# A two-layer trunk in f32 on one core: SBUF tiles moved to multiples of 512 bytes, the pool maps multiplied in plain f32, and late parts, sums and turns placed behind the blocks that follow

## The chip, the cores and the metric

The kernel runs on one core of one Trainium2 chip. The metric is the device time of one execution in microseconds (us), as the median of several runs. The other numbers come from one profiled execution of the same program, in which every engine's instructions carry a start and a duration.

## The reference, cut to what matters

256 tokens of 2048 channels pass through two layers. All of it is f32.

```
x += pool_mixer(rms_norm(x))          # 4 groups of 512 channels: trailing mean minus token, 512x512 map, scale
x += mlp(rms_norm(x))                 # layer 0: 2048 -> 8192, squared relu, 8192 -> 2048
k, v = rms_norm(x) @ w_kv             # 2048 -> 4096
x += attention(rms_norm(x) @ w_q, k, v) @ w_o   # 16 heads of 128, stick-breaking, strictly causal
x += mlp(rms_norm(x))                 # layer 1
return rms_norm(x)
```

## The kernel before, in words

**Products in parts.** A matmul in the format f32r, which keeps fewer bits of an f32 number, is one record in the trace, where a matmul in plain f32 is two. Each f32 value is therefore held as a high part and a low part, and a product is three matmuls: high by high, low by high, high by low. One token tile of 128 rows against 512 weight columns is one matmul; in most products the activations are the stationary operand (loaded into the array, 128 columns) and the weights are the moving one (512 columns). `by_token` (L264) does this for plain products: L271, L273 and L274 are the three matmuls. In `product` (L459, L461, L463) and `whole` (L507, L509, L510) they are the same three for the up product of the MLP.

**Weights.** Every block of weights is 512x512 f32 (1 MB), loaded by a DMA into a `raw` tile or into one of four `chain` tiles (c0, c1, d0, d1), cast to its high part by ScalarE (L194) and subtracted to its low part by VectorE (L195). `hi` and `lo` have three buffers each. `next_block` hands out the next block; loads and splits run ahead of it. The four chain tiles also hold activations where no chain of weights needs them: the parts for K, Q and V, some parts for the up product (d1), and in the head the parts of the pool mixer's input.

**Stages.** The head (pool mixer) does four products of one block each (`product_a(..., groups=1)`), mixes each with a band matrix over the tokens (`mixed`, L625 and L627, plain f32), makes the parts for the up product (`Fast.make`) and turns the stream to token rows (`by_tokens`, L640). Then `mlp` walks the plan of `stage_plan`: group 0 has eight whole blocks U; groups 1 to 7 have the blocks P of a fast product of seven sums in place of eight (stationary tiles fh and fl), with the turns T (transposes of the hidden values to ht0 and ht1, squared) and the down blocks D of the group before; the last group has only T and D, and after each finished chunk of 512 channels the norm that follows takes that chunk (`follow.take(n)`: squares, transposes L333, parts). Then come the K and Q products (`product_w`, here the weights are the stationary operand), V, the attention as side work between blocks, the O product (16 blocks with oT0 to oT3 stationary, `norm1.take(n)` after each chunk), layer 1's MLP and the last norm.

**Order.** Each engine runs its instructions in program order; a scheduler places side work and the split of later blocks between the matmuls, and semaphores hold an instruction until what it reads is there. The SP queue issues nearly all weight loads; loads that add onto a chain tile are issued by GpSimd.

**Tile addresses.** Tiles are laid in each partition one after another, in the order in which the pools are opened, so a small tile moves every tile that follows. From the order and the sizes of the pools, the addresses modulo 512 bytes are: 96 for raw, chain, hi, lo and the stream xr; 256 for what lies behind them on the left (ht0, ht1, the c tiles, oT, attention); 480 for the pools on the right (fh, fl, the last norm). Pieces inside these tiles lie at multiples of 512 bytes, so each stationary piece has its tile's offset.

Of the kernel before, what the change touches and what calls it, by code (L numbers as in the profile page):

```python
# [35 lines left out]
WARM = 12  # L36
# [34 lines left out]
def trunk_kernel(ctx: ExitStack, tc: tile.TileContext, xt_in, band, cols, pool_w, up_w, down_w,  # L71
# [13 lines left out]
    small = ctx.enter_context(tc.tile_pool(name="small", bufs=1))  # L85
    ps_w = ctx.enter_context(tc.tile_pool(name="ps_w", bufs=4, space=PSUM))
# [28 lines left out]
    eps = const.tile([P, 1], F32, name="eps")  # L115
# [12 lines left out]

    for g in range(NCH):
        block(pool_w[g])  # L130
# [33 lines left out]
    def load():  # L164
# [5 lines left out]
        if base is None:  # L170
            raw = wide(tag) if tag else wraw.tile([P, KT, NB], F32, name="raw")
            step = KT // 2 if i < NCH else KT
            for k in range(0, KT, step):
                nc.sync.dma_start(raw[:, k:k + step, :], src[:, k:k + step, :])
# [9 lines left out]
    def split():  # L184
# [6 lines left out]
        if gain is None:  # L191
            step = KT // 2 if i < NCH else KT
            for k in range(0, KT, step):
                nc.scalar.copy(out=hi[:, k:k + step, :], in_=raw[:, k:k + step, :])  # L194
                nc.vector.tensor_tensor(out=lo[:, k:k + step, :], in0=raw[:, k:k + step, :],  # L195
                                        in1=hi[:, k:k + step, :].bitcast(F32), op=ALU.subtract)
# [111 lines left out]
    class Norm:  # L308
        def __init__(self):
            self.parts = [None] * NCH  # L310
            self.ss = small.tile([P, NT, NCH], F32, name="ss", bufs=2)
# [24 lines left out]
        def rows(self):  # L336

            total = small.tile([P, NT], F32, name="total")
# [34 lines left out]
    class Fast(Norm):  # L373
# [3 lines left out]
        def __init__(self, gain, new_bank):  # L377
            super().__init__()
            self.gain, self.new_bank, self.pools = gain, new_bank, []

# [4 lines left out]
        def make(self, n, src=None):  # L385

# [7 lines left out]
            tiles = []  # L394
            for half in range(2):
                if src is None:
                    bank = self.turned(n, half, (0, 1))
                for k in range(2):
                    c = 2 * half + k
                    gs = gt[:, self.gain, n * KT + c:n * KT + c + 1]  # L400
                    if src is None:
                        x = bank[:, :, k, :]
                    else:
                        x = src[:, c, :].rearrange("p (t s) -> p t s", t=NT)
                    tiles.append((half, k, x, gs))
                    to = [(x, hi[:, 1:3, k, :], lo[:, 1:3, k, :])] if half else [
                        (x[:, 0], hi[:, 0, k, :], lo[:, 0, k, :]),
                        (x[:, 1], self.other[:, n, 0, k, :], self.other[:, n, 1, k, :])]
                    for x, h, l in to:
                        nc.scalar.activation(out=h, in_=x, func=AF.Copy, scale=gs)  # L410
                        nc.vector.scalar_tensor_tensor(out=l, in0=x, scalar=gs, in1=h.bitcast(F32),
                                                       op0=ALU.mult, op1=ALU.subtract)

            f = wide(("c0", "c1", "d0", "c0")[n]).rearrange("p a (b k s) -> p (a b) k s", b=2, k=2)
            for half, k, x, gs in tiles:
                nc.scalar.activation(out=f[:, 2 * half:2 * half + 2, k, :], in_=x, func=AF.Copy,
                                     scale=gs)
# [18 lines left out]
    def mlp(layer, norm, following):  # L436

        with scope(name=f"h{layer}", bufs=1) as hp, scope(name=f"ev{layer}", bufs=1) as ev, \
                scope(name=f"ps_s{layer}", bufs=1, space=PSUM) as ps_s:
            spare = cycle(("turn", "x", "y", "z"))  # L440
            new_bank = lambda: ps_s.tile([P, NB], F32, name=next(spare))
# [3 lines left out]
            def product(i, part):  # L445
# [22 lines left out]
                def new(name):  # L468
                    u[name] = hp.tile([P, NB], F32, name=f"c{name}")
                    return u[name]  # L470

                def relu(name):
                    t = int(name[1]) - 1
                    nc.scalar.activation(out=u[name], in_=u[name], func=AF.Relu,
                                         scale=r[:, t:t + 1])
# [16 lines left out]
            def whole(i, j, part):  # L492
# [7 lines left out]
                for t in range(NT):  # L500
# [11 lines left out]
                    if ends:  # L512
                        c = u[f"{i + 1}{t + 1}"] = hp.tile([P, NB], F32, name=f"c{i + 1}{t + 1}")
                        nc.scalar.activation(out=c, in_=b, func=AF.Relu, scale=norm.r[:, t:t + 1])

            def turn(i):

                a, ks = i // 2, slice(2 * (i % 2), 2 * (i % 2) + 2)
                if i % 2 == 0:
                    h[a] = hp.tile([P, KT, 2 * S], F32R, name=f"ht{a}")  # L520
                b = ps_s.tile([P, NB], F32, name="turn").rearrange("p (k s) -> p k s", k=2)
# [6 lines left out]
                q = ev.tile([P, 2, S], F32, name="q")  # L528
# [4 lines left out]
            def down(n, part, follow):  # L533
# [3 lines left out]
                if part == 1:  # L537
# [3 lines left out]
                    if follow is not None:  # L541
                        follow.take(n)

            r = norm.r
            for g in range(NG + 1):
# [4 lines left out]
                for what, *at in stage_plan(g):  # L550
                    if what == "P":
                        product(*at)
                    elif what == "T":
                        turn(*at)
# [8 lines left out]
    with scope(name="ps_p", bufs=1, space=PSUM) as ps_m:  # L563
        new_bank = lambda: ps_m.tile([P, NB], F32, name="turn", bufs=2)
        norm = Fast(G["mlp0"], new_bank)
        pools = [tc.alloc_tile_pool(name=f"xs{n}", bufs=1, reuse_waits="tile")
                 for n in reversed(range(2, NCH))]
# [360 lines left out]
```

## Time and profile before

| | |
|---|---|
| median of 3 runs | 1886.88 us (1886.84 to 1887.16) |
| profiled execution, whole | 1889.27 us |
| its span, first to last instruction | 1887.6 us |
| TensorE busy | 1842.6 us (98%), 8360 records |
| VectorE, ScalarE, GpSimd busy | 70%, 58%, 5% |
| mean granted TensorE clock | 0.987 of full speed |

A record of the profile is one matmul as the engine runs it: a plain f32 matmul has two records, an f32r one has one. The busy time of TensorE says little by itself, since matmuls overlap in the pipe; what counts is the time from one matmul's start to the next one's. The granted clock of a stretch is 1.00 at 2.4 GHz and 0.50 at 1.2 GHz.

### The profile page before, as it was taken

The page shows a single profiled execution, that of the slowest core. Times are in us where ns is not written, and L with a number is a line of the kernel's source. Part 1 is how long each engine was busy: PE and PEld are TensorE (multiplying, and loading weights), DVE is VectorE, ACT ScalarE, POOL GpSimd, SP SyncE. Part 2 cuts the span into 40 slices and gives each one's busy share as a digit, 9 for nine tenths or more (in the row PEclk, how much of TensorE's full clock was granted, in tenths as well). Part 3 has the DMA queues.
Part 4 walks back from the last instruction along what each step waited for, and adds up shares of the span by engine and source line. Part 5 has one row for each costly group of instructions (what it writes and reads, how often), then busy time and mean ns, then how long its engine had stood idle before and what let it go on. Part 6 is the DMA issues. An engine that isn't in the chain of part 4 may idle for free.

```text
span 1887.6 us, 20963 instructions
## 1 busy us (share of the span) xinstructions
PE 1842.6 (98%) x8360; PEld 1494.1 (79%) x8360; DVE 1312.1 (70%) x1134; ACT 1089.5 (58%) x1137; POOL 92.6 (5%) x125
## 2 busy tenths in 40 slices
PE   7899999999999999999999998999999999999987
PEld 5788888888888887888888786888888888888875
DVE  7676777778787765666766566577786877777753
ACT  7655656656565654565665555556565656656553
POOL 0000100000000100000000100000000100000000
PEclk8999999999999998999999999999999999999998
DMA  7479888888879764555445455697979888888741
GB/s 285 138 188 298 195 287 206 271 245 245 257 211 286 200 202 159 179 170 174 169 163 188 159 173 210 192 256 223 268 207 303 191 286 203 278 244 242 183 178 67
DMA packets 57697, 404.85 MB, mean 214 GB/s; under 512 B 6528, under 2 KB 6784, under 8 KB 9472
## 3 DMA queue, kind: packets, MB, share of 16 engines
q1 hardware_dynamic: 45504, 315.44, 46.6%
q0 software_dynamic: 12096, 88.09, 24.4%
q8 instruction: 65, 1.06, 0.2%
q14 instruction: 32, 0.26, 0.0%
HBM read 401.40 MB, written 2.10 MB: 214 GB/s over the span
## 4 chain that ended last, share of the span: by engine, by line
PE 94%; DVE 2%; ACT 1%; issue 1%; DMA 0%; SPq 0%; POOL 0%; DVEq 0%; ACTq 0%; POOLq 0%
PE bank L273 16%; PE bank L271 16%; PE bank L274 16%; PE bank L237 6%; PE x L459 4%; PE x L461 4%; PE x L463 4%; PE bank L242 3%; PE z L463 3%; PE y L463 3%; PE y L461 3%; PE y L459 3%; PE z L461 3%; PE z L459 3%; PE turn L525 2%
## 5 line engine op out<-in xcount | busy, mean ns | idle before, releaser
L195 DVE TENSOR_TENSOR lo<-raw,hi 128x2048 fp32r<-128x2048 f32 (+1 forms) x196 | 440.5, 2247 | 278.8 <-ACT hi L194 278.8
L194 ACT CAST hi<-raw 128x2048 fp32r<-128x2048 f32 (+1 forms) x196 | 367.7, 1876 | 344.7 <-PE bank L273 229.6
L274 PE MATMUL bank<-lo,ht 128*128 128x512 f32 x1024 | 407.9, 398 | 0.0
L271 PE MATMUL bank<-hi,ht 128*128 128x512 f32 x1024 | 405.8, 397 | 1.4 <-ACT ht L527 1.4
L273 PE MATMUL bank<-hi,ht 128*128 128x512 f32 x1024 | 406.7, 397 | 0.0
L195 DVE TENSOR_TENSOR lo<-c,hi 128x2048 fp32r<-128x2048 f32 x112 | 256.5, 2290 | 61.0 <-ACT hi L194 61.0
L194 ACT CAST hi<-c 128x2048 fp32r<-128x2048 f32 x112 | 214.4, 1914 | 134.2 <-PE bank L273 44.4
L273 PEld LDWEIGHTS bank<-hi,ht 128*128 128x128 f32 x1024 | 193.2, 189 | 51.3 <-DVE ht L530 3.6
L271 PEld LDWEIGHTS bank<-hi,ht 128*128 128x128 f32 x1024 | 193.7, 189 | 47.9 <-ACT ht L527 2.2
L274 PEld LDWEIGHTS bank<-lo,ht 128*128 128x128 f32 x1024 | 193.0, 188 | 44.8
L202 DVE SCALAR_TENSOR_TENSOR lo<-raw,gt,hi 128x512 fp32r<-128x512 f32 x192 | 135.4, 753 | 78.0 <-ACT hi L201 77.5
L201 ACT ACTIVATE hi<-raw,gt 128x512 fp32r<-128x512 f32 x192 | 126.0, 715 | 97.0 <-PE bank L237 49.4
L194 ACT CAST hi<-d 128x2048 fp32r<-128x2048 f32 x56 | 107.0, 1911 | 98.9 <-PE bank L273 78.2
L195 DVE TENSOR_TENSOR lo<-d,hi 128x2048 fp32r<-128x2048 f32 x56 | 128.4, 2292 | 45.6 <-ACT hi L194 45.6
L461 PE MATMUL x<-hi,fl 128*128 128x512 f32 x336 | 133.7, 398 | 0.0
L459 PE MATMUL x<-hi,fh 128*128 128x512 f32 x336 | 133.7, 398 | 0.0
L463 PE MATMUL x<-lo,fh 128*128 128x512 f32 x336 | 133.0, 396 | 0.0
L539 DVE TENSOR_TENSOR xr<-bank,xr 128x512 f32<-128x512 f32 x128 | 88.0, 687 | 51.0 <-PE bank L274 51.0
L180 POOL DMA_DIRECT2D c<-in_up_w x56 | 48.5, 866 | 923.5 <-DVE lo L195 876.1
L237 PE MATMUL bank<-d,hi 128*128 128x512 f32 x256 | 90.3, 396 | 0.0
L459 PE MATMUL z<-hi,fh 128*128 128x512 f32 x224 | 90.3, 403 | 0.0
L237 PE MATMUL bank<-c,hi 128*128 128x512 f32 x256 | 89.0, 396 | 0.0
(248 smaller groups left out, 2856.7 us busy)
## 6 DMA issues: line engine op xcount, KB each, us to landing
raw<-in_down_w SPq DMA_DIRECT2D x128, 1024.0 KB, 5.0
c<-in_up_w POOLq DMA_DIRECT2D x56, 1024.0 KB, 10.4
raw<-in_up_w SPq DMA_DIRECT2D x44, 1024.0 KB, 5.4
c<-in_up_w SPq DMA_DIRECT2D x28, 1024.0 KB, 5.0
d<-in_up_w SPq DMA_DIRECT2D x28, 1024.0 KB, 7.5
d<-in_up_w POOLq DMA_DIRECT2D x28, 1024.0 KB, 8.6
raw<-in_k_w SPq DMA_DIRECT2D x16, 1024.0 KB, 4.8
raw<-in_q_w SPq DMA_DIRECT2D x16, 1024.0 KB, 4.8
```

The source lines that it names most:

```text
L194: nc.scalar.copy(out=hi[:, k:k + step, :], in_=raw[:, k:k + step, :])
L195: nc.vector.tensor_tensor(out=lo[:, k:k + step, :], in0=raw[:, k:k + step, :], in1=hi[:, k:k + step, :].bitcast(F32), op=ALU.subtract)
L201: nc.scalar.activation(out=hi[:, k, :], in_=raw[:, k, :], func=AF.Copy, scale=gs)
L202: nc.vector.scalar_tensor_tensor(out=lo[:, k, :], in0=raw[:, k, :], scalar=gs, in1=hi[:, k, :].bitcast(F32), op0=ALU.mult, op1=ALU.subtract)
L237: nc.tensor.matmul(banks[j], lhsT=hi[:, k, cols], rhs=a, start=first, stop=last)
L271: nc.tensor.matmul(banks[t], lhsT=a_hi, rhs=hi[:, k, :], start=first and k == 0, stop=False)
L273: nc.tensor.matmul(banks[t], lhsT=a_lo, rhs=hi[:, k, :], start=False, stop=False)
L274: nc.tensor.matmul(banks[t], lhsT=a_hi, rhs=lo[:, k, :], start=False, stop=last and k == KT - 1)
L459: nc.tensor.matmul(b, lhsT=ah, rhs=wh, start=begins and kg == 0 and k == 0, stop=False, skip_group_check=True)
L461: nc.tensor.matmul(b, lhsT=al, rhs=wh, start=False, stop=False, skip_group_check=True)
L463: nc.tensor.matmul(b, lhsT=ah, rhs=wl, start=False, stop=ends, skip_group_check=True)
L539: nc.vector.tensor_tensor(out=chunk(t, n), in0=bank["d"][t], in1=chunk(t, n), op=ALU.add)
```

## The change

- **Addresses.** `eps` is a piece of a tile of 448 bytes, `ss` and `total` are pieces of tiles of 128 and 192 bytes, and a tile of 480 bytes (`edge`) stands at the right end. By the order and sizes of the pools, raw, chain, hi, lo, xr, ht, oT, the attention's tiles, fh and fl then all begin at multiples of 512 bytes. The constants (ident, ones) stay where they were.
- **Pool maps.** The product of a group with its map is plain f32: 8 matmuls of 512 columns (L672) in place of 24 in parts. The map is loaded straight into a buffer of `hi` or `lo`. The casts and subtractions of map and stream go; the stream is scaled by the norm's gain in 16 VectorE instructions (`gained`). 16 warm-up matmuls stand in place of 12.
- **Head.** `Fast.make` becomes `quarters` (four evacuations into f, three casts, three subtractions) and `sums`. Chunks 2 and 3 are mixed behind U000 (`rest`), and turned to token rows behind U010 (`tokens_of_rest`).
- **Last group of a layer.** The turns go through four banks in rotation (turn, x, y, z) in place of one, and the plan is T0 T1 D00 T2 T3 D01.
- **The last chunk of a norm.** In layer 0 `follow.take(3)` becomes side work behind the block that follows; in layer 1 `norm1.take(3)` becomes side work behind U000. The banks of PSUM change hands at `end_of_attention` for that.

```diff
-        order = "T2 T3 T0 T1 D00 D01 D10 D11 D20 D21 D30 D31"
+        order = "T0 T1 D00 T2 T3 D01 D10 D11 D20 D21 D30 D31"
...
+    edge = ctx.enter_context(tc.tile_pool(name="edge", bufs=1, side="right"))
+    nc.vector.memset(edge.tile([P, EDGE], F32, name="edge"), 0.0)
...
-    eps = const.tile([P, 1], F32, name="eps")
+    eps = const.tile([P, 112], F32, name="eps")[:, 0:1]
...
+        def quarters(self, n, src=None):
...
+            f = self.f[n] = wide(self.homes[n]).rearrange("p a (b k s) -> p (a b) k s", b=2, k=2)
...
+                    nc.scalar.activation(out=f[:, 2 * half:2 * half + 2, k, :], in_=x, func=AF.Copy,
+                                         scale=gt[:, self.gain, n * KT + c:n * KT + c + 1])
+            for h, l, x in ((hi[:, 0], lo[:, 0], f[:, 0]),
+                            (self.other[:, n, 0], self.other[:, n, 1], f[:, 1]),
+                            (hi[:, 1:3], lo[:, 1:3], f[:, 2:4])):
+                nc.scalar.copy(out=h, in_=x)
+                nc.vector.tensor_tensor(out=l, in0=x, in1=h.bitcast(F32), op=ALU.subtract)
...
-                b = ps_s.tile([P, NB], F32, name="turn").rearrange("p (k s) -> p k s", k=2)
+                b = new_bank() if last else ps_s.tile([P, NB], F32, name="turn")
...
-                    if follow is not None:
+                    if follow is not None and n == NCH - 1 and layer == 0:
+                        side.append([lambda: follow.take(n)])
+                    elif follow is not None:
                         follow.take(n)
...
+    def load_map(g):
+        pool, name = ((whi, "hi"), (wlo, "lo"))[g % 2]
+        w[g] = pool.tile([P, KT, NB], F32, name=name)
+        step = KT // 2
+        for k in range(0, KT, step):
+            nc.sync.dma_start(w[g][:, k:k + step, :], pool_w[g, :, k:k + step, :])
+
+    def product(g):
+
+        ys[g] = [pp.tile([P, NB], F32, name=f"y{t}") for t in range(NT)]
+        for t in range(NT):
+            bank = ps_w.tile([P, NB], F32, name="bank")
+            for k in range(KT):
+                nc.tensor.matmul(bank, lhsT=xg[g][:, k, t * P:(t + 1) * P], rhs=w[g][:, k, :],
+                                 start=k == 0, stop=k == KT - 1)
+            nc.scalar.copy(out=ys[g][t], in_=bank)
...
+    product(0)
+    scaled_bands()
+    product(1)
+    mixed(0)
+    norm.sums(0)
+    product(2)
+    mixed(1)
+    norm.sums(1)
+    by_tokens(0)
+    product(3)
+    by_tokens(1)
+    early.release()
...
+    side.extend([[rest], [tokens_of_rest]])
...
+    side.append([lambda: norm1.take(NCH - 1)])
```

Three places show how instructions move on TensorE. A row gives the line, the operation, what it writes and reads, and the semaphores it waits for (DVE is VectorE, Activation is ScalarE).

The first is the end of the head. Before, the last band products (mix) and turns (xs) of chunks 2 and 3 stand ahead of the first block U000, which is the row L507:

```order
L625 MATMUL mix_569<-bands_135,y0_409 128x256 [waits DVE_49]
L627 MATMUL mix_569<-bands_135,y1_410 128x128
L640 MATMUL turn_620<-ident_85,xs_130 128x128
L640 MATMUL turn_626<-ident_85,xs_130 128x128 [waits Activation_49]
L640 MATMUL turn_626<-ident_85,xs_130 128x128 x2
L640 MATMUL turn_620<-ident_85,xs_130 128x128 [waits DVE_49]
L640 MATMUL turn_626<-ident_85,xs_130 128x128
L507 MATMUL x_659<-hi_334,fh_384 128x512
```

Now the turns of chunk 1 (xs1) are the last ahead of U000 (L516), and chunk 2's band products (L634, into z and turn) stand behind its 24 matmuls:

```order
L672 MATMUL bank_369<-lo_166,c1_149 128x512 x3
L649 MATMUL z_375<-ident_90,xs1_146 128x128 [waits Activation_49]
...
L649 MATMUL turn_381<-ident_90,xs1_146 128x128 [waits Activation_49]
...
L516 MATMUL x_392<-hi_394,fh_276 128x512
L518 MATMUL x_392<-hi_394,fl_277 128x512
...
L634 MATMUL z_440<-bands_141,y0_295 128x256 [waits Activation_49]
L636 MATMUL z_440<-bands_141,y1_296 128x128
L634 MATMUL turn_447<-bands_141,y0_295 128x256 [waits Activation_49]
...
L516 MATMUL x_392<-hi_400,fh_276 128x512
```

What moved is the work of two of the four chunks: it stands behind a block that does not read it.

The second place is the last group of layer 0, right after block D31 of the group before. Before, all turns write the one bank `turn`, and a turn waits for ScalarE to have read the one ahead:

```order
L274 MATMUL bank_4715<-lo_4748,ht1_4259 128x512
L525 MATMUL turn_4823<-ident_85,c21_4314 128x128 [waits PE_49]
...
L525 MATMUL turn_4832<-ident_85,c21_4314 128x128 [waits PE_49,Activation_49]
...
L525 MATMUL turn_4842<-ident_85,c11_4371 128x128 [waits PE_49,Activation_49]
...
L271 MATMUL bank_4860<-hi_4765,ht0_4841 128x512 [waits Activation_49]
L271 MATMUL bank_4861<-hi_4765,ht0_4841 128x512
L271 MATMUL bank_4947<-hi_4862,ht0_4841 128x512 [waits DVE_49]
L525 MATMUL turn_4851<-ident_85,c11_4371 128x128 [waits PE_49,Activation_49]
```

Now the four turns write four banks, one behind the other, and D00 follows (L267 and L269 are its first two kinds of matmul, high and low part of ht0):

```order
L270 MATMUL bank_4583<-lo_4616,ht1_4127 128x512
L536 MATMUL turn_4691<-ident_90,c11_4239 128x128 [waits PE_49,Activation_49]
...
L536 MATMUL x_4700<-ident_90,c11_4239 128x128
...
L536 MATMUL y_4742<-ident_90,c21_4182 128x128
...
L536 MATMUL z_4751<-ident_90,c21_4182 128x128 [waits DVE_49]
...
L267 MATMUL bank_4709<-hi_4633,ht0_4690 128x512 [waits Activation_49]
...
L267 MATMUL bank_4815<-hi_4711,ht0_4690 128x512 [waits DVE_49]
L267 MATMUL bank_4816<-hi_4711,ht0_4690 128x512 [waits DVE_49]
L269 MATMUL bank_4709<-hi_4633,ht0_4690 128x512 [waits DVE_49]
```

No turn waits for a read of the turn ahead any more; the one wait for VectorE that D00 keeps is the low part of ht0.

The third place is the end of the O product, ahead of layer 1's MLP. Before, the last chunk's transposes (bank_m) stand between O's last matmul and U000 (L507), which waits for ScalarE:

```order
L274 MATMUL bank_8239<-lo_8271,oT3_5243 128x512
L333 MATMUL bank_m_8372<-ident_85,xr0_118 128x128 [waits DVE_49]
...
L333 MATMUL bank_m_8385<-ident_85,xr0_118 128x128 [waits Activation_49]
...
L333 MATMUL bank_m_8372<-ident_85,xr1_119 128x128 [waits DVE_49]
...
L507 MATMUL x_8425<-hi_8300,fh_7871 128x512 [waits PE_49,Activation_49]
```

Now U000 (L516 to L519) follows O's last matmul, and the transposes of chunk 3 (L330) stand behind it, ahead of U010:

```order
L270 MATMUL bank_8092<-lo_8124,oT3_5072 128x512
L516 MATMUL x_8216<-hi_8153,fh_7742 128x512 [waits Activation_49]
L518 MATMUL x_8216<-hi_8153,fl_7743 128x512
L519 MATMUL x_8216<-lo_8154,fh_7742 128x512 [waits DVE_49]
...
L330 MATMUL z_8258<-ident_90,xr0_127 128x128 [waits DVE_49]
...
L330 MATMUL turn_8265<-ident_90,xr0_127 128x128 [waits PE_49]
...
L516 MATMUL x_8216<-hi_8183,fh_7742 128x512 [waits Activation_49]
```

What moved is the whole of `take(3)`: its transposes, parts and sums lie beside two blocks.

## Rows read from the trace of the kernel before

**Rows 1.** The page: span, and busy time by engine.
```profile
span 1887.6 us, 20963 instructions
PE 1842.6 (98%) x8360; PEld 1494.1 (79%) x8360; DVE 1312.1 (70%) x1134; ACT 1089.5 (58%) x1137; POOL 92.6 (5%) x125
```

**Rows 2.** TensorE's groups: line, operation, out<-in, count; busy us, mean ns; idle before.
```profile
L271 PE MATMUL bank<-hi,ht 128*128 128x512 f32 x1024 | 405.8, 397 | 1.4 <-ACT ht L527 1.4
L459 PE MATMUL x<-hi,fh 128*128 128x512 f32 x336 | 133.7, 398 | 0.0
L459 PE MATMUL z<-hi,fh 128*128 128x512 f32 x224 | 90.3, 403 | 0.0
L273 PE MATMUL bank<-hi,oT 128*128 128x512 f32 x128 | 51.0, 399 | 0.0
L507 PE MATMUL x<-hi,fh 128*128 128x512 f32 x32 | 13.8, 430 | 5.5 <-ACT c L416 5.5
```

**Rows 3.** Windows: busy (count) of PE, PEld, DVE, ACT, POOL; clock, DMA, GB/s.
```profile
889.54:894.98 5.44, 5.44 (x25) 4.50 (x24) 4.13 (x7) 2.84 (x5) 0.00 (x0) 1.00 0.43 173
79.73:82.45 2.72, 2.72 (x13) 2.25 (x12) 1.43 (x1) 0.02 (x1) 0.00 (x0) 1.00 0.29 39
82.45:90.82 8.37, 8.37 (x37) 6.79 (x36) 3.15 (x2) 5.07 (x4) 0.00 (x0) 1.00 0.64 234
1092.10:1108.89 16.79, 16.79 (x73) 13.51 (x72) 11.11 (x14) 9.77 (x16) 0.00 (x0) 1.00 0.51 164
403.02:408.62 5.60, 5.60 (x25) 4.51 (x24) 3.17 (x2) 3.83 (x3) 0.00 (x0) 1.00 1.08 228
408.62:414.22 5.60, 5.60 (x25) 4.50 (x24) 4.31 (x3) 2.40 (x3) 0.00 (x0) 1.00 1.00 246
```

**Rows 4.** Timeline of TensorE beside attention: start us, us, instruction.
```profile
821.46 0.59 PE L752 MATMUL bank_m<-qT,kT 128*128 128x256 f32 x2
821.89 0.38 PE L754 MATMUL bank_m<-qT,kT 128*128 128x128 f32 x2
...
847.42 0.40 PE L237 MATMUL bank<-c,hi 128*128 128x512 f32 x1
847.66 0.28 PE L242 MATMUL bank<-c,lo 128*128 128x256 f32 x1
847.77 0.39 PE L237 MATMUL bank<-c,hi 128*128 128x512 f32 x1
```

**Rows 5.** Timeline of the head: first cast and matmul, and U000.
```profile
8.86 1.04 ACT L194 CAST hi<-raw 128x1024 fp32r<-128x1024 f32 x1 [1.47 <-DMA raw<-in_pool_w]
...
9.96 0.80 PE L271 MATMUL bank<-hi,d 128*128 128x512 f32 x1 [4.57 <-ACT hi L194]
...
65.78 0.48 PE L507 MATMUL x<-hi,fh 128*128 128x512 f32 x1
```

**Rows 6.** TensorE's waits: line, whom it waited for, us, times, longest.
```profile
PE turn L525 <- ACT q L529: 8.2, 4, 2.3
PE mix L625 <- DVE xs L630: 8.1, 11, 2.3
PE x L507 <- ACT c L416: 5.5, 1, 5.5
```

**Rows 7.** Windows around the waits, columns as in rows 3.
```profile
706.00:731.00 25.00, 20.39 (x79) 15.83 (x78) 11.32 (x11) 10.08 (x12) 0.00 (x0) 0.80 0.42 161
1157.00:1172.00 15.00, 9.12 (x34) 6.96 (x34) 10.49 (x20) 8.20 (x18) 0.00 (x0) 0.77 0.59 212
1812.00:1831.00 19.00, 14.05 (x55) 10.79 (x54) 7.20 (x8) 6.75 (x10) 0.00 (x0) 0.82 0.42 159
```

**Rows 8.** Chain of waits at layer 0's last group: start us, us, what.
```profile
710.93 1.91 ACT hi L194
...
712.86 2.29 DVE lo L195
715.15 0.61 DVE ht L530
```

More of the change, by code (lines that the diff above doesn't have):

```diff
@@ L191, in split @@
         if gain is None:
[L192 to L196, printed above, removed]
+            nc.scalar.copy(out=hi, in_=raw)
+            nc.vector.tensor_tensor(out=lo, in0=raw, in1=hi.bitcast(F32), op=ALU.subtract)
         else:
@@ L399, in make, with sums @@
                     c = 2 * half + k
[L400 to L417, printed above, removed]
+                    x = bank[:, :, k, :] if src is None else src[:, c, :].rearrange(
+                        "p (t s) -> p t s", t=NT)
+                    nc.scalar.activation(out=f[:, 2 * half:2 * half + 2, k, :], in_=x, func=AF.Copy,
[5 more added lines that the diff above has]
+                nc.vector.tensor_tensor(out=l, in0=x, in1=h.bitcast(F32), op=ALU.subtract)
+        def sums(self, n):
+            f, (hi, lo) = self.f[n], self.parts[n]
             for i in range(2):
@@ new lines, in trunk_kernel, with gained @@
+    xs = [early.tile([P, KT, S], F32, name=f"xs{n}") for n in range(2)] + xs
+    squares = early.tile([P, 2, S], F32, name="squares")
+    pairs = [wide("c0"), wide("c1")]
+    xg = [pairs[n // 2][:, :, n % 2 * S:(n % 2 + 1) * S] for n in range(NCH)]
+    w, ys = [None] * NCH, [None] * NCH
+    def gained(n):
+        for k in range(KT):
+            c = n * KT + k
+            nc.vector.tensor_scalar(out=xg[n][:, k, :], in0=xs[n][:, k, :],
+                                    scalar1=gt[:, G["pool"], c:c + 1], scalar2=None, op0=ALU.mult)
@@ new lines, in by_tokens, with load_stream @@
+    def by_tokens(g):
+        for t in range(NT):
+            bank = new_bank()
+            for k in range(KT):
+                nc.tensor.transpose(bank[:, k * P:(k + 1) * P], xs[g][:, k, t * P:(t + 1) * P],
+                                    ident)
+            nc.scalar.copy(out=chunk(t, g), in_=bank)
+        norm.squares(g)
+    def load_stream(n, pieces=1):
+        step = KT // pieces
+        for k in range(0, KT, step):
+            nc.sync.dma_start(xs[n][:, k:k + step, :], xt_in[n, :, k:k + step, :])
@@ new lines, in trunk_kernel @@
+    nc.sync.dma_start(gt, cols)
+    load_stream(0, 2)
+    load_map(0)
+    for n in range(1, NCH):
+        load_stream(n)
+    load_map(1)
+    nc.sync.dma_start(bands, band)
+    for n in range(2, NCH):
+        load_map(n)
+    for n in range(NCH):
+        gained(n)
+        all_squares(n)
+    load()
+    product(0)
[10 more added lines that the diff above has]
+    early.release()
@@ new lines, in rest, with tokens_of_rest, new_pair @@
+    def rest():
+        for g in range(2, NCH):
+            mixed(g)
+        for g in range(2, NCH):
+            norm.sums(g)
+    def tokens_of_rest():
+        for g in range(2, NCH):
+            by_tokens(g)
+        norm.rows()
+        while pools:
+            pools.pop().release()
+    side.extend([[rest], [tokens_of_rest]])
+    kvq = mlp(0, norm, lambda new_bank: Plain(new_bank), ps_s)
+    ps_m = []
+    def new_pair():
+        return ps_m[0].tile([P, 2, NB], F32, name="bank_m")
@@ new lines, in trunk_kernel, with end_of_attention, added @@
+    norm1 = Fast(G["mlp1"], None, ("c0", "c1", "d0", "c0"))
+    last_banks = []
+    def end_of_attention():
+        attention.close()
+        ps_m[0].release()
+        last_banks.append(four_banks(1))
+        norm1.new_bank = bank_of(last_banks[0], ("z", "turn"))
+    side.append([end_of_attention])
+    for n in range(NCH):
+        def added(t, bank, n=n):
+            nc.vector.tensor_tensor(out=chunk(t, n), in0=bank, in1=chunk(t, n), op=ALU.add)
+        product_a(oT, added)
+        if n < NCH - 1:
```

453 lines of the change are left out of this document (201 added, 252 removed).

## The prediction

> **What bounds the kernel now.** I read the page's first block, then TensorE's groups, then windows that hold nothing but matmuls of one kind, then TensorE's waits and the windows around them. TensorE is busy for 98% of the span, so time can only come from shorter matmuls or from its few idle stretches [rows 1]. The waits name three large stretches: the turns of the last groups (8.2 us), the band products of the head (8.1 us) and the first up block of layer 1 (5.5 us) [rows 6]. A stretch costs more than its wait, since the granted clock falls behind it: 0.77 to 0.82 on the mean of these windows against 1.00 in steady work [rows 3, 7].
>
> The larger matter is the steady pace. In each window all matmuls are f32r of 512 columns, and the weight loads (PEld) count them, so the length over that count is the time from one start to the next. The moving operand is always a weight tile at offset 96 modulo 512 bytes; only the stationary one differs. With a chain tile (96): 5.44 us / 24 = 226.7 ns for V, and 2.72 / 12 = 226.7 for the part of an up block that reads d1. With fh and fl (480): 8.37 / 36 = 232.5 in the same kind of block, and 5.60 / 24 = 233.3 in P (the window from 403.02). With oT (256): 16.79 / 72 = 233.2, and with ht (256), in a down block, 5.60 / 24 = 233.3 (the window from 408.62) [rows 3]. So the pace follows the stationary tile's address, by 6 to 7 ns of 230, while the DMA share varies from 0.29 to 1.08 without a matching trend.
>
> **The sum, part by part.**
>
> *Addresses.* After the change every f32r operand of these products lies at offset 0, stationary and moving alike. The trace has no such pair. Its nearest rows are those of equal offsets, 96 with 96, at 226.7 ns; the slow pairs have unequal ones. I take 226.7 for all. The counts [rows 2]: ht 3 x 1024 = 3072, at 6.6 ns 20.3 us; P 3 x (336 + 224 + 224) = 2352, the y group being as large as the z group shown, at 6.6 ns 15.5 us; oT 3 x 128 = 384 at 6.5 ns, 2.5 us; fh and fl in U 3 x (32 + 32 + 16 + 16) = 288 at 5.8 ns, 1.7 us. Together -40.0 us. The bounds: nothing, if the gap has another cause; and on the good side the pace of a matmul that loses nothing. The two records of a plain f32 matmul of 256 columns take 0.43 us [rows 4], 0.215 each, which is 516 cycles at 2.4 GHz or two a column; I take 215 ns as what 512 undisturbed cycles cost. All 6096 matmuls at 215 would be (233.2 - 215) x 6096 = 111 us, and the products that are at 227 now give some 6 us more for V and d1 and up to 14 us for K and Q. What speaks against equal offsets as the whole rule is K and Q: both operands at 96, and yet a pair of 512 and 256 columns takes 0.35 us [rows 4], about 27 ns over 768 such cycles. What lies above 215 ns is therefore open, and the range must hold it.
>
> *The head.* Before, the first half map is there at 8.86, the first matmul starts at 9.96, U000 at 65.78 [rows 5], and with two blocks of 24 x 232.5 ns, U001 would start at 76.9. The work of all four chunks is behind TensorE in both orders only at U001, so I compare there. A f32 matmul of 256 columns takes 0.43 us [rows 4], so one of 512 takes 0.86; 32 of them are 27.6 us, against 96 x 0.227 = 21.8 before: the maps alone cost 5.8 us more on TensorE. But nothing stands ahead of them save the map's arrival and the gain: no cast, no split. From 8.9: maps 27.6; four mixes of 4 x (0.43 + 0.22) = 10.4 [rows 4]; the turns of four chunks, 8 records of 0.11 each, 3.6; U000 and U010, 2 x 24 x 0.23 = 11.1. That is 61.6. I add 2.7 us for a stretch at half clock, since the engine starts with a gap as before, 3.5 us for waits that remain (turns of chunk 1 on ScalarE's copies, mix 2 on its first band product, U001 on the casts of chunk 2 and 3), 0.2 for the sums: 68.0, so -9 us. Bounds: -14 if no wait remains, -4 if the eleven waits of band products [rows 6] keep half their 8.1 us and the clock falls a second time. ScalarE and VectorE lose their parts of stream and maps, so they are no later than now.
>
> *The last groups.* In layer 0 D31 ends at 710.9; the cast of the next block (1.91), its split on VectorE (2.29), the low part of ht (0.61) and four turns through one bank follow in a row [rows 8]. The window of 25 us holds 79 records [rows 7], 16 turns of 0.11 and 63 matmuls of 0.233, 16.4 us of steady work: 8.6 us are lost, part as waits and part at a clock of 0.80. Layer 1's window loses 19 - 10.9 = 8.1 in the same way. Now sixteen turns of 0.11 run at once (1.8 us), while ScalarE still makes the 1.91 us cast that is queued ahead of its reads; the high part of ht0 is there 2.5 us behind D31, four matmuls follow, and the low part comes only when VectorE is through the 2.29 us split and its own 0.61: 4.9 us behind D31. TensorE does 2.7 us of work in those 4.9, so about 2.2 us stay; if the clock falls again, 1.8 more. That is -6.4 and -5.9, -12.3 in all; bounds -8 and -16.
>
> *O to the MLP of layer 1.* Before, the window of 15 us holds 34 records [rows 7], 8 transposes and 26 matmuls, 6.9 us of steady work: 8.1 us lost, at a clock of 0.77. Behind the change U000 follows O's last matmul; its own inputs (chunks 0 and 1) are long made. The cover for chunk 3's parts is U000 and U010, 11.1 us, against the 5.5 us that the old U000 waited for them [rows 6]. I count -8.1; if the cover failed it would be -3. In layer 0 the same step lies behind the first K block, where none of the three large waits stands [rows 6]; I count nothing, its cover being that block's 64 matmuls.
>
> The tail and the attention stay. Sum: -40.0 - 9 - 12.3 - 8.1 = -69.4 us. From the profiled execution's 1889.27 that is 1819.9; that execution stands 2.4 us above the median, so 1817 us for the median.
>
> The Trainium skill's page "SBUF — State Buffer", in "Who interferes with whom", gives TensorE read ports of its own for moving data and for weight loads, and says that nobody makes it wait. By that an address could not matter, and -40 would be nothing: the third case below. The trace differs so far: 226.7 against 232.5 ns within the same sort of block, one beside the other [rows 3]. The page "TensorE: Matmul & The Clock Gate", in "Back-to-back issue gap", gives columns over the clock plus about 2.5 ns, so 216 ns for 512 columns; no f32r window here shows it, and the second case goes towards it.
>
> **The rivals.**
>
> *The excess goes, not only the gap.* If the 11 ns that 96 with 96 still has above 215 come from the offset itself, offset 0 takes them as well. For it: each slow and each fast pair here begins off a multiple of 512. Against it: no row. A pace of 221 gives 6 x 6576 = 39 us more than mine (6576 with V and d1), 1778; 215 gives 77 and up to 14 at K and Q, 1726.
>
> *Address does nothing.* The pace belongs to the kind of tile, not to its offset. Only the stalls are won: -29.4, so 1857. For it: each kind of tile has one offset, so the trace cannot part the two. Against it: d1 and fh are read in like pieces by the same line.
>
> *The stalls stay.* The change does not do what it says: the last groups wait for the same cast and split, U000 of layer 1 waits at its second block. With half of the 29.4 kept, 1832.
>
> *Slower.* Offset 0 for both operands and for all that ScalarE and VectorE read and write puts every access on one place, and TensorE's reads collide more than now. The stalls won, 29.4 us, are lost again when the 6576 matmuls run at (6096 x 233.2 + 480 x 226.7 + 29400) / 6576 = 237.2 ns. Placed as far above 233.3 as that is above 226.7, at 240, the cost is 41.5 + 6.4 - 29.4 = +18.5 us, 1905. For it: K and Q, equal offsets and still slow [rows 4]. Against it: V at 96 with 96 is the fastest of all.
>
> **How the numbers follow.** Mine 40% (1803 to 1830 with the bounds of head and last groups); the excess goes too 30%; address does nothing 17%; stalls stay 7%; slower 6%. The predicted time is the likeliest case's 1817. The range of 1728 to 1862 leaves out the slower case, the lowest end of the second and the highest of the third. A change of 0.2%, 3.8 us, is about what a measurement here tells from none; faster 0.94, same 0.02, slower 0.04, since the slower case just reaches over that bound in part.
>
> **What would show it.** A window of down blocks: 24 matmuls in 5.44 us is mine, 5.2 the second case, 5.60 the third, above 5.7 the slower one. U001 near 68 us. The waits of the turns for q gone, one wait of some 1.5 us for the low part of ht0 in each layer. No idle stretch between O and U000. I am wrong if down and P blocks part again in pace, or if the first up blocks wait for chunks 2 and 3.

## The result, and the profile after

The changed kernel takes 1820.85 us (median, 1819.81 to 1822.87) against 1887.02 for the kernel before: a ratio of 0.9649, 95% interval 0.9632 to 0.9666. The forecast was 1817 us. The profiled execution took 1822.87 us.

The first lines of the page of the changed kernel, which answer to [rows 1]: the span is 66.4 us shorter, TensorE is busy for 41 us less.

```profile
span 1821.2 us, 20807 instructions
PE 1801.2 (99%) x8332; PEld 1480.2 (81%) x8332; DVE 1295.5 (71%) x1103; ACT 1069.1 (59%) x1089; POOL 92.5 (5%) x125
```

Windows of the changed kernel with the columns of [rows 3]: a P block, a down block, a V block, and the d1 part of an up block.

```profile
1190.59:1196.03 5.44, 5.44 (x26) 4.50 (x24) 5.13 (x4) 3.81 (x2) 0.86 (x1) 1.00 0.96 178
1196.03:1201.47 5.44, 5.44 (x26) 4.50 (x24) 3.83 (x2) 2.42 (x3) 1.73 (x2) 1.00 1.00 262
927.72:933.16 5.44, 5.44 (x25) 4.50 (x24) 4.12 (x7) 2.92 (x5) 0.00 (x0) 1.00 0.43 166
1136.92:1139.64 2.72, 2.72 (x14) 2.25 (x13) 2.62 (x2) 0.14 (x2) 0.00 (x0) 1.00 0.28 36
```

The 24 matmuls of the first three take 5.44 us and the 12 of the last one 2.72, 226.7 ns each. Before, only V and d1 had that pace; P and down took 5.60.

TensorE's waits (line, whom it waited for, us in total, times, longest) have lost the three large ones of [rows 6]. These are the waits that the changed kernel has at the places of the change:

```profile
PE bank L269 <- DVE ht L541: 2.4, 2, 1.2
PE bank L267 <- ACT ht L538: 1.1, 2, 0.5
PE bank L672 <- DMA hi<-in_pool_w: 1.0, 1, 1.0
```

The head of the changed kernel, from TensorE's timeline (start us, us, instruction): the maps begin, the second map begins, U000 begins, U001 begins. They answer to [rows 5].

```profile
8.82 7.11 PE L672 MATMUL bank<-hi,c 128*128 128x512 f32 x16 [1.02 <-DMA hi<-in_pool_w]
15.76 6.17 PE L672 MATMUL bank<-lo,c 128*128 128x512 f32 x14
...
43.77 0.48 PE L516 MATMUL x<-hi,fh 128*128 128x512 f32 x1
...
61.33 0.48 PE L516 MATMUL x<-hi,fh 128*128 128x512 f32 x1
```

The first map's 16 records take 15.76 - 8.82 = 6.94 us, 0.434 each, which is the price that two records of 256 columns had [rows 4]. U001 starts at 61.33, not at 68.

The last group of layer 0 in the changed kernel: the window of the length of the first one in [rows 7], and TensorE's timeline there.

```profile
674.00:699.00 25.00, 23.25 (x106) 18.81 (x104) 15.40 (x14) 13.04 (x16) 0.00 (x0) 0.93 0.50 174
```

```profile
684.07 1.23 PE L267 MATMUL bank<-hi,ht 128*128 128x512 f32 x4 [0.55 <-ACT ht L538]
686.50 0.79 PE L269 MATMUL bank<-hi,ht 128*128 128x512 f32 x1 [1.20 <-DVE ht L541]
687.10 0.63 PE L270 MATMUL bank<-lo,ht 128*128 128x512 f32 x1
687.52 0.63 PE L267 MATMUL bank<-hi,ht 128*128 128x512 f32 x1
```

In a window of equal length are 106 records in place of 79. (The two windows do not begin at quite the same matmul; the table below compares the stages from end to end.) Two waits are left, 0.55 and 1.20 us, and behind the second the matmuls start 0.42 us apart: the granted clock is 0.50 from 686.5 to 689.9 us, for 3.4 us.

The end of the O product: U000 starts 0.23 us behind O's last matmul, without a wait.

```profile
1122.16 0.39 PE L270 MATMUL bank<-lo,oT 128*128 128x512 f32 x1
1122.39 0.39 PE L516 MATMUL x<-hi,fh 128*128 128x512 f32 x1
```

Where the 66 us come from is seen when the starts of the first and last matmuls of each stage are read from three timelines: before, the kernel before with the new addresses alone (first experiment), and the changed kernel. A last group is counted from the last P matmul, so the block D31 belongs to it. Stage lengths in us, from one profiled execution each:

| from TensorE's starts | before | addresses alone | changed |
|---|---|---|---|
| start to the first P block | 110.3 | 107.2 | 95.1 |
| P blocks of layer 0 | 594.8 | 580.7 | 580.9 |
| last group of layer 0 | 64.5 | 62.7 | 58.0 |
| K, Q, V and attention | 295.4 | 295.9 | 295.9 |
| O | 94.6 | 92.4 | 92.4 |
| O's end to the first P block of layer 1 | 53.9 | 52.5 | 44.7 |
| P blocks of layer 1 | 594.9 | 580.9 | 580.8 |
| last group of layer 1 and tail | 69.5 | 69.0 | 64.2 |
| all | 1877.9 | 1841.3 | 1811.8 |

So the run with the addresses alone is 36.6 us shorter, and the rest of the change gives 12.1 more in the head, 9.6 more in the two last groups, and 7.8 more on the way from O to the P blocks.

Not all of the 36.6 is pace. 2.2 us of it stand ahead of U000, where no fast tile, ht or oT is read yet. These are the windows up to U000, before and with the addresses alone; the clock was at 0.87 in the one and at 0.95 in the other:

```profile
0.00:65.78 65.78, 50.73 (x208) 37.69 (x209) 52.27 (x106) 52.52 (x103) 1.35 (x9) 0.87 0.63 224
0.00:63.55 63.55, 48.40 (x208) 35.52 (x209) 52.46 (x107) 52.38 (x103) 1.33 (x9) 0.95 0.64 232
```

From U000 on the addresses give 34.4 us, which agrees with the 34.2 between the medians below.

### The profile page after: what moved, and what is told of

It is laid out like the page before. It is cut to its first block, busy times and chain, and to the rows that moved or that the text cites. A ratio compares the mean times of both kernels' runs of the same rounds, so it can differ in the third digit from the quotient of the medians.

```text
span 1821.2 us, 20807 instructions
## 1 busy us (share of the span) xinstructions
PE 1801.2 (99%) x8332; PEld 1480.2 (81%) x8332; DVE 1295.5 (71%) x1103; ACT 1069.1 (59%) x1089; POOL 92.5 (5%) x125
## 4 chain that ended last, share of the span: by engine, by line
PE 97%; DVE 1%; issue 1%; ACT 0%; DMA 0%; SPq 0%; POOL 0%; DVEq 0%; ACTq 0%; POOLq 0%
PE bank L269 16%; PE bank L270 16%; PE bank L267 16%; PE bank L233 7%; PE x L468 4%; PE x L470 4%; PE x L472 4%; PE bank L238 3%; PE z L472 3%; PE z L468 3%; PE z L470 3%; PE y L468 3%; PE y L472 3%; PE y L470 3%; PE bank L672 2%; PE turn L536 1%
## 5 line engine op out<-in xcount | busy, mean ns | idle before, releaser
L192 DVE TENSOR_TENSOR lo<-raw,hi 128x2048 fp32r<-128x2048 f32 x188 | 430.7, 2291 | 251.2 <-ACT hi L191 250.5
L191 ACT CAST hi<-raw 128x2048 fp32r<-128x2048 f32 x188 | 359.7, 1913 | 310.8 <-PE bank L269 227.8
L269 PE MATMUL bank<-hi,ht 128*128 128x512 f32 x1024 | 401.9, 393 | 2.4 <-DVE ht L541 2.4
L270 PE MATMUL bank<-lo,ht 128*128 128x512 f32 x1024 | 400.5, 391 | 0.0
L267 PE MATMUL bank<-hi,ht 128*128 128x512 f32 x1024 | 399.4, 391 | 1.1 <-ACT ht L538 1.1
L269 PEld LDWEIGHTS bank<-hi,ht 128*128 128x128 f32 x1024 | 193.0, 188 | 47.4 <-DVE ht L541 7.9
L267 PEld LDWEIGHTS bank<-hi,ht 128*128 128x128 f32 x1024 | 192.9, 189 | 41.4 <-ACT ht L538 1.6
L191 ACT CAST hi<-d 128x2048 fp32r<-128x2048 f32 x56 | 107.1, 1913 | 92.4 <-PE bank L269 73.3
```

Source lines behind the costliest of these rows:

```text
L191: nc.scalar.copy(out=hi, in_=raw)
L192: nc.vector.tensor_tensor(out=lo, in0=raw, in1=hi.bitcast(F32), op=ALU.subtract)
L267: nc.tensor.matmul(banks[t], lhsT=a_hi, rhs=hi[:, k, :], start=first and k == 0, stop=False)
L269: nc.tensor.matmul(banks[t], lhsT=a_lo, rhs=hi[:, k, :], start=False, stop=False)
L270: nc.tensor.matmul(banks[t], lhsT=a_hi, rhs=lo[:, k, :], start=False, stop=last and k == KT - 1)
```

## The experiments

**The addresses alone.** The kernel before, with only the paddings:

```diff
+EDGE = 120
...
+    edge = ctx.enter_context(tc.tile_pool(name="edge", bufs=1, side="right"))
...
-    eps = const.tile([P, 1], F32, name="eps")
+    eps = const.tile([P, 112], F32, name="eps")[:, 0:1]
...
-            total = small.tile([P, NT], F32, name="total")
+            total = small.tile([P, 48], F32, name="total")[:, 0:NT]
```

> The kernel before, with only the paddings of the change (eps, ss, total, edge), so that every f32r tile begins at a multiple of 512 bytes; order, maps and turns are as before. Theory: the pace of each f32r matmul of 512 columns falls to about 227 ns (24 matmuls of a down block in 5.44 us in place of 5.60), so the addresses alone give 34 to 40 us: 1847 to 1853 us. Rival (the pace belongs to the kind of tile, and the change's gain lies in its moved work): 1884 to 1888 us, down blocks at 5.60.

1853.59 us against 1887.83 before; ratio 0.9825 (0.9809 to 0.9842). A down block of this kernel, and the three waits that the rest of the change removes:

```profile
1220.58:1226.02 5.44, 5.44 (x26) 4.51 (x24) 3.83 (x2) 2.43 (x3) 1.73 (x2) 1.00 1.03 279
```

```profile
PE mix L629 <- DVE xs L634: 9.6, 13, 2.3
PE turn L529 <- ACT q L533: 8.1, 4, 2.3
PE x L511 <- ACT c L420: 5.6, 1, 5.6
```

The pace is a matter of the addresses, and the three waits are still there. The rival that the pace belongs to the kind of tile has fallen.

**Which addresses.** These are five runs of the changed kernel with other paddings; all offsets are modulo 512 bytes. The first has all tiles at 96, the second ht, oT, fh and fl at 256 with the weights at 0, the third the weights, ht, oT, fh and fl at 256 with the chain tiles at 0:

```diff
# all at 96
-EDGE = 120
+EDGE = 96
...
-    eps = const.tile([P, 112], F32, name="eps")[:, 0:1]
+    eps = const.tile([P, 136], F32, name="eps")[:, 0:1]
# stationary at 256
-EDGE = 120
+EDGE = 56
...
-            total = small.tile([P, 48], F32, name="total")[:, 0:NT]
+            total = small.tile([P, 112], F32, name="total")[:, 0:NT]
# weights at 256
-EDGE = 120
+EDGE = 56
...
+    gap = ctx.enter_context(tc.tile_pool(name="gap", bufs=1))
+    nc.vector.memset(gap.tile([P, 64], F32, name="gap"), 0.0)
     whi = ctx.enter_context(tc.tile_pool(name="whi", bufs=3))
```

> The changed kernel with every f32r tile, stationary and moving, shifted by 96 bytes, so that all are at 96 modulo 512. Theory (what counts is that both operands have the same offset): the pace stays at 227 ns, down block 5.44 us, time 1818 to 1824 us. Rival (what counts is to begin at a multiple of 512): down block 5.55 to 5.6 us or more, time 1845 to 1860 us.

> The changed kernel with ht, oT and the fast tiles shifted by 256 bytes; weights and chain tiles stay at 0. Theory (same offset): 233 ns for down, P and O, so 6096 matmuls lose about 6 ns each, 1853 to 1860 us; V and the d1 part of the up blocks stay at 227 ns. Rival 1 (only the moving operand's offset counts): nothing changes, 1818 to 1824 us. Rival 2 (only the stationary operand's offset to a multiple of 512 counts): as the theory here, to be told apart by the runs with 96 and with the weights moved.

> The changed kernel with hi, lo, ht, oT and the fast tiles at 256; only raw and the chain tiles (V's stationary tiles and d1) stay at 0. Theory (same offset): down, P and O at 227 ns; V and d1, now 0 against 256, go to 231 to 233, 480 matmuls by 6 ns: 1821 to 1827 us. Rival (multiple of 512 counts): down, P and O slow, V partly: 1850 us or more.

Measured 1821.76, 1819.53 and 1823.64 us in one run each, so none differs from the changed kernel. A down block of the run at 96, of the run with the stationary tiles at 256, and of the run with the weights at 256, with that run's d1 part (0 against 256) behind it:

```profile
1194.74:1200.18 5.44, 5.44 (x26) 4.50 (x24) 3.83 (x2) 2.43 (x3) 1.72 (x2) 1.00 1.02 268
```

```profile
1194.18:1199.62 5.44, 5.44 (x25) 4.50 (x24) 3.83 (x2) 2.42 (x3) 1.72 (x2) 1.00 1.01 268
```

```profile
1196.78:1202.22 5.44, 5.44 (x26) 4.50 (x24) 3.83 (x2) 2.42 (x3) 1.72 (x2) 1.00 1.02 271
1125.86:1128.59 2.73, 2.73 (x13) 2.20 (x12) 2.23 (x6) 0.53 (x3) 0.00 (x0) 1.00 0.36 69
```

Multiples of 512 are not needed: 96 with 96 is as fast. My theory, the same offset, fell in the second and third run: 256 against 0 costs nothing. What was slow before had offsets 160 and 384 apart. Two more runs moved the stationary tiles by such amounts, ht and oT through `total`, fh and fl through `EDGE` (128 and 160 in the first, whose edit is shown; 64 and 384 in the second, with `EDGE` at 24 and a `total` of 64):

```diff
-EDGE = 120
+EDGE = 80
...
-            total = small.tile([P, 48], F32, name="total")[:, 0:NT]
+            total = small.tile([P, 80], F32, name="total")[:, 0:NT]
```

> The changed kernel with ht and oT at 128 and the fast tiles at 160 modulo 512; weights and chain tiles at 0. The runs so far: 226.7 ns for (stationary, moving) = (0, 0), (96, 96), (256, 0), (0, 256), (256, 256); 233 for (256, 96) and (480, 96), differences of 160 and 384. Theory (the difference modulo 256 counts): both groups slow, down and O at 228 to 233 and P at 233 ns, 1845 to 1860 us. Rival (a moving operand off a multiple of 64 or 128 bytes costs time unless the stationary one shares its offset, the difference itself does not count): both at 227 ns, 1818 to 1824 us.

> The changed kernel with ht and oT at 64 and the fast tiles at 384 modulo 512; weights and chain tiles at 0. Theory (the difference modulo 256 counts): P at 232 to 233 ns, as before at a difference of 384; down and O between 227 and 233; 1835 to 1860 us. Rival (only a moving operand off a multiple of 64 or 128 bytes costs): both at 227 ns, 1818 to 1824 us.

1853.62 and 1854.31 us. First a down block (128) and a P block (160) of the one, then a down block (64) and a P block (384) of the other:

```profile
1213.61:1219.21 5.60, 5.60 (x26) 4.51 (x24) 3.73 (x2) 2.43 (x3) 1.72 (x2) 1.00 1.02 282
1208.01:1213.61 5.60, 5.60 (x26) 4.51 (x24) 5.05 (x4) 3.78 (x2) 0.86 (x1) 1.00 0.96 167
```

```profile
1215.15:1220.74 5.59, 5.59 (x26) 4.49 (x24) 3.76 (x2) 2.43 (x3) 1.73 (x2) 1.00 1.01 278
1209.57:1215.15 5.58, 5.58 (x26) 4.52 (x24) 5.04 (x4) 3.80 (x2) 0.86 (x1) 1.00 0.94 162
```

All eleven pairs tried fit one sentence: whole blocks run at 226.7 ns where the stationary and the moving tile lie a multiple of 256 bytes apart (0 or 256), and at 232 to 233 ns where they lie 64, 128, 160 or 384 apart. Differences under 64 bytes were not tried, and why 256 is the number stays open. Some 33 us of the kernel hang on it (1853.6 and 1854.3, one run each, against 1820.85).

The pair is not all that sets the pace. In the changed kernel every whole P block that no turns interrupt runs at 226.7 ns (70 blocks; before, 233.0 on the mean), but the pieces of 10 to 12 matmuls into which turns split the other P blocks run at up to 231.4, 229.6 on the mean (before, 232.6). One such piece behind a turn, its second and its last matmul, ten starts in 2.31 us:

```profile
266.37 0.40 PE L470 MATMUL z<-hi,fl 128*128 128x512 f32 x1
...
268.68 0.39 PE L472 MATMUL z<-lo,fh 128*128 128x512 f32 x1
```

**The last groups as before.** The old plan and the one bank:

```diff
-        order = "T0 T1 D00 T2 T3 D01 D10 D11 D20 D21 D30 D31"
+        order = "T2 T3 T0 T1 D00 D01 D10 D11 D20 D21 D30 D31"
...
-                        turn(*at, g == NG)
+                        turn(*at, False)
```

> The changed kernel with the last group of each layer as before: plan T2 T3 T0 T1 D00 D01, and all turns through the one bank. Theory (turns that wait for ScalarE's read of the one bank, and the half clock behind them): about 5 us more in each layer, 1829 to 1833 us, with four waits of the turns for q of up to 2.3 us and a half clock of 7 to 10 us behind each. Rival (the cast and the split ahead on ScalarE and VectorE set the time, whatever the order of the turns): at most 3 us more, 1821 to 1824.

1830.07 us (1829.36 and 1830.78), 9.2 above the changed kernel. The four waits are back:

```profile
PE turn L536 <- ACT q L540: 8.5, 4, 2.3
```

The theory holds; its rival would have shown at most 3 us. Which of the two does it, the order or the four banks, was not tried apart.

**take(3) ahead of layer 1's MLP, and the banks.** First the parts of chunk 3 straight behind the O product, then the same with the four banks given out only behind them:

```diff
# take(3) ahead
-        if n < NCH - 1:
-            norm1.take(n)
-    op.release()
-    side.append([lambda: norm1.take(NCH - 1)])
+        if n == NCH - 1:
+            op.release()
+        norm1.take(n)
# and the banks behind
-        ps_m[0].release()
-        last_banks.append(four_banks(1))
-        norm1.new_bank = bank_of(last_banks[0], ("z", "turn"))
+        norm1.new_bank = lambda: new_pair()[:, 0, :]
...
+    ps_m[0].release()
+    last_banks.append(four_banks(1))
```

> The changed kernel with norm1's last chunk taken straight behind the O product, ahead of layer 1's U000, as before; the four banks of PSUM are still given out ahead of the O product. Theory (the place of the transposes and parts of chunk 3 decides): U000 starts 6 to 7 us behind O's last matmul, 1828 to 1831 us. Rival (the banks decide: U000 writes x and y, chunk 3 uses z and turn, so U000 need not wait for ScalarE's reads of chunk 3): U000 starts at most 2 us behind O's end, 1820 to 1824 us.

> The changed kernel with norm1's last chunk taken straight behind the O product, as in the run with take(3) ahead, and with the four banks of layer 1 given out only behind it, so that U000's bank x lies where chunk 3's transposes are still read, as before. Theory (the banks decide): TensorE waits 3 to 6 us at U000 for ScalarE's four reads of chunk 3 behind its 1.91 us cast, and the clock falls to half behind that wait: 1825 to 1830 us. Rival (the shorter evacuation into f is what freed U000, wherever the banks lie): a wait under 2 us, 1820 to 1823 us.

The first took 1821.41 us, no more than the changed kernel. TensorE's timeline shows U000 0.59 us behind O's last matmul, with the transposes between its first matmuls:

```profile
1122.63 0.40 PE L270 MATMUL bank<-lo,oT 128*128 128x512 f32 x1
1122.86 0.38 PE L330 MATMUL z<-ident,xr 128*128 128x128 f32 x2
1123.08 0.38 PE L330 MATMUL turn<-ident,xr 128*128 128x128 f32 x2
1123.22 0.48 PE L516 MATMUL x<-hi,fh 128*128 128x512 f32 x1
```

The second took 1826.76 us, which is in the theory's range. But its U000 waits only 1.71 us, which is the rival's sign, and the clock does not fall behind that wait:

```profile
1124.54 0.40 PE L270 MATMUL bank<-lo,oT 128*128 128x512 f32 x1
...
1128.08 0.50 PE L516 MATMUL x<-hi,fh 128*128 128x512 f32 x1 [1.71 <-ACT c L405]
```

From O's last matmul to the first P block are 52.5 us with the addresses alone, 47.2 here, 44.8 with take(3) ahead and own banks, 44.7 in the changed kernel. So of the 7.8 us at this place 5.3 come with the rest of the change, 2.4 from the banks, and 0.1 from the deferral, given the banks. What the rest of the change has at this place is that ScalarE reads chunk 3's banks four times, where before ScalarE's casts and evacuations read them ten times and VectorE six times: the wait of U000 is 1.71 us in place of 5.6, and the half clock behind it is gone. That this reading is the cause was not tried by itself, and neither was the deferral without the banks. That this run's total is 5.9 us above the changed kernel's is more than the 2.5 us seen here; the head of its profiled execution is 2.2 us longer, with a wait of 1.94 us for the first map and 3.4 us at half clock behind it.

**The head.** All four chunks mixed and turned in the head, and 12 warm-up matmuls in place of 16:

```diff
-    side.extend([[rest], [tokens_of_rest]])
+    rest()
+    tokens_of_rest()
# 12 warm-ups, and apart from it
-WARM = 16
+WARM = 12
```

> The changed kernel with chunks 2 and 3 mixed, summed and turned to token rows in the head, not as side work behind U000 and U010. Theory (both blocks cover VectorE's and ScalarE's work on chunks 2 and 3): waits of the band products for VectorE's writes come back on TensorE, the first group is through 4 to 6 us later, 1825 to 1828 us. Rival (the scheduler fills the gaps between them with matmuls of the first blocks anyway, and the maps alone made the head shorter): 1819 to 1823 us.

> The changed kernel with 12 warm-up matmuls in place of 16. Theory (the head keeps its clock because the warm-up reaches to 7.8 us and TensorE then waits only 1 us): TensorE is idle from about 5.4 to 8.8 us, the clock falls to half for some 7 us behind it, and the first maps take 1.7 us each in place of 0.86: 3 to 4 us more, 1823 to 1827 us. Rival (the 4 more warm-ups do nothing): the granted clock in the first 20 us is 1.00 but for the start, 1819 to 1823 us.

1820.16 and 1821.77 us: neither matters in the total. In the first the head up to the P blocks takes 95.6 us against 95.1: the scheduler lays the same work between the matmuls of the first blocks. U000 starts at 44.24 us there, and chunk 2's and 3's band products and turns stand among its matmuls and those of U010. So this run did not take the cover by these blocks away, and no run did. How the 12.1 us of the head part between the cover and the maps in plain f32, without casts and splits ahead of them, stays open. In the second the clock fell, at a smaller price than expected. Its first map, window and timeline:

```profile
8.79:17.43 8.64, 8.64 (x17) 3.71 (x18) 3.83 (x11) 2.38 (x4) 0.00 (x0) 0.80 1.03 410
```

```profile
8.79 8.80 PE L672 MATMUL bank<-hi,c 128*128 128x512 f32 x16 [2.29 <-DMA hi<-in_pool_w]
17.43 6.17 PE L672 MATMUL bank<-lo,c 128*128 128x512 f32 x14
```

The wait ahead of the maps is 2.29 us in place of 1.02, the clock is at 0.80 over the first map, and it takes 8.64 us in place of 6.94. These 1.7 us are still there at the first P block (96.7 against 95.1), and do not show in the total because in this execution the last groups kept their clock. That the four warm-ups decide is not shown: with 16 of them the wait for the first map was 0.32 to 2.82 us over all profiles, since the clock rose anywhere from 4.3 to 7.2 us and the first map's matmuls could start anywhere from 7.7 to 9.3, and the fall came in one of them too (behind 1.94 us, in the run with the banks behind).

**A version beyond the change.** What is left in the last groups is that ht0 is made behind D31, with a cast and a split queued ahead of it. These are the pieces of the changed kernel's chain at layer 0 between D31 and the low part of ht0:

```profile
681.62 1.91 ACT hi L191
...
683.55 2.29 DVE lo L192
685.85 0.61 DVE ht L541
```

D31 reads only ht1, so the turns to ht0 can stand ahead of it, if the last P blocks come one step earlier (V0 and V1 are the turns T0 and T1, told apart because they rotate through the four banks):

```diff
+        if g == NG - 1:
+            order = order.replace("D30 P20 P21 D31", "P20 P21 D30 V0 V1 D31")
     else:
-        order = "T0 T1 D00 T2 T3 D01 D10 D11 D20 D21 D30 D31"
+        order = "T2 T3 D00 D01 D10 D11 D20 D21 D30 D31"
...
+                    elif what == "V":
+                        turn(*at, True)
```

> A version beyond the change: in the last group that still has P blocks, the order of its end is P20 P21 D30 T0 T1 D31 in place of D30 P20 P21 D31 T0 T1, and T2 T3 stand ahead of D00. Theory (the stall that is left in the last groups, 0.55 and 1.2 us of wait and a half clock of 3.4 us, goes, since D31's 5.4 us cover the cast, the split and the parts of ht0): 3 us less in each layer, 1813 to 1816 us, no half clock near 686 and 1758 us. Rival (the split of the block behind is queued ahead of ht0's low part on VectorE again, or D31's sums on VectorE delay it): the wait only moves to another block, 1819 to 1823 us.

1815.15 us (1814.94 to 1815.68), a ratio of 0.9614 (0.9598 to 0.963) to the kernel before: the fastest of all, 5.7 us under the changed kernel. A window over D30, the turns, D31 and D00 of layer 0, and the turns in the timeline:

```profile
668.00:690.00 22.00, 22.00 (x106) 18.34 (x106) 15.46 (x12) 13.81 (x15) 0.00 (x0) 1.00 0.77 273
```

```profile
676.46 0.60 PE L538 MATMUL turn<-ident,c 128*128 128x128 f32 x4
...
682.82 0.60 PE L538 MATMUL y<-ident,c 128*128 128x128 f32 x4
```

TensorE is busy for all of the 22 us at full clock.

## Why the prediction was right, and where its terms were off

The total was 4 us off, but only because terms went both ways: that it came so near is in part luck.

- **Addresses:** forecast -40.0, measured -36.6 from the start to the last matmul, 2.2 of which stand ahead of U000 and go with the clock there; -34.4 from U000 on, and -34.2 on the medians of the two runs. The pace of 226.7 was right for ht, whose mean from one start to the next (neighbours, full clock) fell from 233.4 to 226.9, and for whole P blocks. Too large was the gain in P: with the pieces between turns its mean fell from 232.9 to 227.4, 5.5 ns and not 6.6, which is 2.6 us of what is missing; the rest was not traced. The reason given, equal offsets, was nearly right: it is equality modulo 256, as far as the pairs tried show. The second case (the excess over 215 goes as well) did not come: no window at 0 is under 226.7.
- **Head:** forecast -9, measured -12.1 up to the P blocks beside the addresses; by the forecast's own measure, U001 from 76.9 to 61.33, it is -15.6. The bare sum was 61.6 for U001, and it starts at 61.33. The 6.2 us that I added for a half clock and for waits are the term that failed: the only wait is the 1.02 us for the first map, and the clock stays at full speed. Two of the other runs show that a part of them can come: with the clock at half over the first map their heads are 1.7 and 2.2 us longer. That no wait of chunks 2 and 3 is left fits the cover that the forecast wanted, but no run took the cover away.
- **Last groups:** forecast -12.3, measured -9.6 beside the addresses. The waits that stay, 0.55 and 1.20 us for each layer, were forecast as 2.2 together. The clock fell to half behind them in both layers of the profiled execution, which was named at 1.8 us for each layer but not counted. In the runs with the head in one piece and with 12 warm-ups, whose last groups are the same, it did not fall, and the group of layer 0 takes 56.5 us in place of 58.0, that of layer 1 62.6 in place of 64.2; with them the gain beside the addresses would be 12.7.
- **O to the MLP:** forecast -8.1, measured -7.8. The size was right and the reason was not: the forecast had U000 and U010 cover the work that moved behind them, and with its own banks U000 starts as early without that move, which gave 0.1 us. The banks gave 2.4 us; the other 5.3 come with the rest of the change, most likely the fewer reads of the banks.
- **K, Q, V, attention:** forecast no change, measured +0.5.

## What to carry to other kernels

Where the two operands of such f32r matmuls lie in SBUF, look at how far apart they start modulo 256 bytes: a small tile more or less in front of a pool shifts every tile behind it, and here 64 bytes and more cost or gave 3% of each matmul. When a wait is removed, ask of each piece of the edit which one frees the waiting instruction; here the moved work added nothing to what the banks that it moved with gave. A short wait that is left behind may still cost nearly as much again in clock (here 1.75 us of waits and 1.5 us of clock in each last group); cover it with a block that doesn't read what is being made.

## What the runs showed of the hardware that was not expected

- In whole blocks an f32r matmul of 512 columns with a weight load beside it takes 226.7 ns where the stationary and the moving tile are a multiple of 256 bytes apart, and 232 to 233 ns at 64, 128, 160 and 384 bytes. Behind turns within a block it takes up to 231.4 ns at a fast pair as well. It does not matter whether either begins at a multiple of 512.
- At no offset did a block come down to the 215 ns of one record of an f32 matmul of 256 columns. What the other 11 ns are stays open. K and Q, with both operands at 0, kept their pace: that stage is as long as before.
- The Trainium skill's "SBUF — State Buffer", in "Who interferes with whom", has TensorE wait for nobody on its two read ports. Here the pace depends on where the two operands lie relative to each other: 5.60 against 5.44 us for the same block at two paddings. Where in the engine or the memory that arises, no run shows.
- The length of a wait did not decide alone whether the clock fell. The same 1.20 us in the last group were followed by 3.4 us at half clock in some runs and by none in others; ahead of the first map, 1.94 and 2.29 us were, and four waits of 2.33 to 2.82 us were not.
